# Forming the adaLN modulation's products on ScalarE and GpSimd instead of TensorE, in a two-layer RG-LRU and pooling trunk

## The chip, the cores and the metric

The kernel runs on one core of one Trainium2 chip. The core has TensorE (PE in the profile; its weight loads are listed apart as PEld), VectorE (DVE), ScalarE (ACT), GpSimd (POOL) and SyncE (SP), which issues nearly all DMAs here. The metric is the device time of one execution in microseconds (us); a time is a median over runs. The kernel before the change took 2298.68 us, median of 3 runs, from 2298.04 to 2298.79.

## The reference

The program is one pass of a small trunk over 640 tokens of width 1024: 512 latent tokens and 128 context tokens. There are two layers; each has a SwiGLU channel mixer, a token mixer (an RG-LRU with two scan directions in layer 0, a multi-window pool in layer 1), and another channel mixer. Each of these three sublayers is modulated by nine vectors per layer, which come from a conditioning vector:

```python
silu_ctx = jax.nn.silu(c_ctx)[None]
silu_lat = jax.nn.silu(c)
for l in range(DEPTH):
    mod_c = silu_ctx @ mod_w[l] + mod_b[l]     # [1, 1024] @ [1024, 9 * 1024]
    mod_s = silu_lat @ mod_w[l] + mod_b[l]
...
def _layer(x, mod, l, norm_g, ffn_w1, ffn_w3, ffn_w2, mixer):
    sh1, sc1, g1, sh2, sc2, g2, sh3, sc3, g3 = jnp.split(mod[:, None, :], N_MOD, axis=-1)
    h = _modulate(_rmsnorm(x, norm_g[l, 0]), sh1, sc1)
    x = x + 0.5 * g1 * _rmsnorm(_swiglu(h, ...), norm_g[l, 1])
    h = _modulate(_rmsnorm(x, norm_g[l, 2]), sh2, sc2)
    y, st = mixer(h)
    x = x + g2 * _rmsnorm(y, norm_g[l, 3])
    ...
```

Everything is float32. The change touches `silu_ctx @ mod_w[l]` and `silu_lat @ mod_w[l]`: two vectors (context and latent, called v = 0 and 1 in the kernel) against a matrix of 1024 x 9216 per layer.

## The kernel before, in words

The large products run as three float32r matmuls each (weights and activations are split exactly into a high and a low part: `wh`, `wl`; `gh`, `gl`; `hh`, `hl`). Weights come in pieces of 128 x 1024 through two buffers called `raw`; ScalarE makes `wh` (L137), VectorE makes `wl` (L138), and six pairs of them are kept ahead.

A channel mixer has 22 features of 128 rows. Per feature TensorE forms two products for token group A (256 tokens, `uvA`, two PSUM buffers) and two for group B (384 tokens, `uB` and `vB`, one PSUM buffer each), all at L326. ScalarE applies SiLU to u (L346), VectorE multiplies by v (L347), ScalarE and VectorE split the result into `gh` and `gl` (L153, L154). After every two features comes a block of 60 matmuls (`block_B`, L366) with the two features of the block before, whose sums go to `yacc` (L372 on ScalarE for the first block, L374 on VectorE after). The last four features are multiplied in `final`, tile by tile, with the norms behind them: `c_res` (a square with sum on ScalarE L280, an epsilon on VectorE L281, a power of -0.5 on GpSimd L283, two VectorE operations L291 and L292), the same statistic of x, a scaling on ScalarE (L298), and `c_h`, which transposes on TensorE (L431), modulates (L437, L439) and splits into `hh` and `hl` for the next sublayer. While the last tiles' norms finish, the next sublayer's first products of group A run.

The modulation of the first channel mixer is computed in `start`. The other 16 chunks of 1024 columns (shift, scale and gate, kinds 0, 1, 2, of the sublayers) come from a generator, `mod_gen`. It is stepped from the phases' code (`mod_step` once after each group of products, 9 steps at the start of a recurrent or channel mixer; `mod_until` before the chunk is needed). A chunk needs eight pieces of 128 x 1024, loaded into two buffers called `mw` on SP's queue; one step takes a piece and multiplies it with four matmuls of 128 x 32 weights and 256 columns, on four column groups of the array (L207). `csil` holds the two conditioning vectors' SiLU in columns 0 and 1 of 32. After eight steps the sums stand in PSUM (`m`, one buffer); a few small operations turn them into per-channel columns `ab` (kinds 0 and 1) or, by L249 and L252, into the broadcast gate `G` (kind 2), of which there is one buffer, so that a gate waits for the phase before to end.

Instructions stand on each engine's queue in an order that a scheduler sets when the program is built, each queue running in that order: an instruction that waits holds back all behind it on its engine. Work of the generator may stand on a queue well ahead of where the program text has it.

## Time and profile before

| | value |
|---|---|
| median of 3 runs | 2298.68 us |
| span of the profiled execution | 2297.5 us |
| PE busy, share of the span | 98% |
| PEld, DVE, ACT, POOL busy | 88%, 47%, 33%, 3% |
| granted TensorE clock, mean | 0.992 |
| DMA, mean of the span | 107 GB/s |

The profiled execution's own time is its span of 2297.5 us plus what lies around it, which the profile does not show; it is 1.2 us below the median of the runs. Busy times are unions of intervals, and matmuls overlap each other, so that a matmul's listed duration (0.28 us for 256 columns) is longer than its share of TensorE's time (one starts each 0.12 us). "Idle before" is what an engine waited for just ahead of an instruction, with the releaser behind the arrow. `x1024` for the modulation's matmuls at L207 counts two records per matmul: there are 512 of them, in 128 steps of four.

### The profile page before, as it was taken

The page shows a single profiled execution, that of the slowest core. Times are in us where ns is not written, and L with a number is a line of the kernel's source. Part 1 is how long each engine was busy: PE and PEld are TensorE (multiplying, and loading weights), DVE is VectorE, ACT ScalarE, POOL GpSimd, SP SyncE. Part 2 cuts the span into 40 slices and gives each one's busy share as a digit, 9 for nine tenths or more (in the row PEclk, how much of TensorE's full clock was granted, in tenths as well). Part 3 has the DMA queues.
Part 4 walks back from the last instruction along what each step waited for, and adds up shares of the span by engine and source line. Part 5 has one row for each costly group of instructions (what it writes and reads, how often), then busy time and mean ns, then how long its engine had stood idle before and what let it go on. Part 6 is the DMA issues. An engine that isn't in the chain of part 4 may idle for free.

```text
span 2297.5 us, 32647 instructions
## 1 busy us (share of the span) xinstructions
PE 2243.3 (98%) x14071; PEld 2024.6 (88%) x14071; DVE 1089.0 (47%) x1570; ACT 753.0 (33%) x1123; POOL 64.9 (3%) x107
## 2 busy tenths in 40 slices
PE   7999999998999999999999999999999899999998
PEld 5999889987888898989998898898897799999997
DVE  5333433346998643343344434334436743343444
ACT  5322112226976622112224421212125732222211
POOL 0000000000111000000000000000000100000000
PEclk9999999999999999999999999999999999999999
DMA  8333343324424344332221433433331322222221
GB/s 280 121 115 119 111 128 112 114 74 147 129 101 142 133 133 125 110 124 74 81 68 55 150 108 109 129 119 120 105 111 45 113 76 74 81 68 87 79 74 46
DMA packets 74288, 246.27 MB, mean 107 GB/s; under 512 B 7568, under 2 KB 15776, under 8 KB 74144
## 3 DMA queue, kind: packets, MB, share of 16 engines
q1 hardware_dynamic: 74112, 244.18, 33.6%
q8 instruction: 110, 1.80, 0.3%
q14 instruction: 34, 0.28, 0.0%
q0 software_dynamic: 32, 0.01, 0.0%
HBM read 238.91 MB, written 5.25 MB: 106 GB/s over the span
## 4 chain that ended last, share of the span: by engine, by line
PE 86%; DVE 6%; ACT 5%; DMA 2%; issue 1%; POOL 1%; SPq 0%; POOLq 0%; ACTq 0%; DVEq 0%
PE b L366 23%; PE uvA L326 22%; PE uB L326 17%; PE vB L326 16%; PE m L207 3%; ACT xp L280 2%; DVE yacc L291 1%; DVE x L292 1%; DVE yacc L374 1%; PE b L573 1%; POOL st L283 1%; DMA mw<-in_mod_w_dram 1%; ACT yacc L298 0%; PE b L746 0%; PE m L249 0%
## 5 line engine op out<-in xcount | busy, mean ns | idle before, releaser
L138 DVE TENSOR_TENSOR wl<-raw,wh 128x1024 fp32r<-128x1024 f32 x294 | 356.5, 1223 | 482.3 <-ACT wh L137 482.3
L137 ACT ACTIVATE wh<-raw 128x1024 fp32r<-128x1024 f32 x270 | 281.1, 1055 | 648.1 <-PE b L366 405.8
L326 PE MATMUL uvA<-hhA,wl 128*128 128x256 f32 x1536 | 440.2, 287 | 1.6 <-ACT xp L532 1.5
L326 PE MATMUL uvA<-hlA,wh 128*128 128x256 f32 x1536 | 435.8, 284 | 0.0
L326 PE MATMUL uvA<-hhA,wh 128*128 128x256 f32 x1536 | 435.3, 284 | 0.0
L366 PE MATMUL b<-wh,gl 128*128 128x512 f32 x960 | 376.6, 392 | 3.4 <-DVE gl L154 1.6
L366 PE MATMUL b<-wl,gh 128*128 128x512 f32 x960 | 375.0, 391 | 0.0
L366 PE MATMUL b<-wh,gh 128*128 128x512 f32 x960 | 374.3, 391 | 0.0
L374 DVE TENSOR_TENSOR yacc<-yacc,b 128x512 f32<-128x512 f32 x380 | 256.0, 686 | 169.7 <-PE b L366 169.6
L326 PEld LDWEIGHTS uvA<-hhA,wl 128*128 128x128 f32 x1536 | 294.3, 192 | 21.9 <-issue 15.4
L326 PEld LDWEIGHTS uvA<-hlA,wh 128*128 128x128 f32 x1536 | 294.8, 192 | 2.1 <-DVE hlB L154 0.4
L326 PEld LDWEIGHTS uvA<-hhA,wh 128*128 128x128 f32 x1536 | 294.7, 192 | 1.6 <-issue 1.6
L326 PE MATMUL uB<-hhB,wl 128*128 128x384 f32 x760 | 259.4, 341 | 0.9 <-ACT hhB L153 0.9
L326 PE MATMUL vB<-hhB,wl 128*128 128x384 f32 x760 | 254.8, 335 | 2.3 <-ACT gt L584 2.3
L326 PE MATMUL uB<-hlB,wh 128*128 128x384 f32 x760 | 254.9, 335 | 0.2
L326 PE MATMUL vB<-hhB,wh 128*128 128x384 f32 x760 | 255.0, 336 | 0.0
L326 PE MATMUL vB<-hlB,wh 128*128 128x384 f32 x760 | 254.9, 335 | 0.0
L326 PE MATMUL uB<-hhB,wh 128*128 128x384 f32 x760 | 254.6, 335 | 0.0
L366 PEld LDWEIGHTS b<-wh,gl 128*128 128x128 f32 x960 | 180.2, 188 | 48.0 <-issue 5.8
L366 PEld LDWEIGHTS b<-wh,gh 128*128 128x128 f32 x960 | 180.2, 188 | 37.6
L366 PEld LDWEIGHTS b<-wl,gh 128*128 128x128 f32 x960 | 180.3, 188 | 36.0
L347 DVE TENSOR_TENSOR r<-r,uvA 128x256 f32<-128x256 f32 x88 | 37.0, 421 | 266.6 <-ACT r L346 266.5
(207 smaller groups left out, 2389.5 us busy)
## 6 DMA issues: line engine op xcount, KB each, us to landing
raw<-in_w_dram SPq DMA_DIRECT2D x264, 512.0 KB, 3.5
mw<-in_mod_w_dram SPq DMA_DIRECT2D x132, 512.0 KB, 3.7
raw<-in_w_in_dram SPq DMA_DIRECT2D x16, 512.0 KB, 3.6
raw<-in_w_out_dram SPq DMA_DIRECT2D x8, 512.0 KB, 3.5
x_spill<-x SPq DMA_DIRECT2D x5, 512.0 KB, 2.6
x<-x_spill SPq DMA_DIRECT2D x5, 512.0 KB, 6.7
x<-in_x_s_dram SPq DMA_DIRECT2D x4, 512.0 KB, 6.3
wl<-in_mod_w_dram SPq DMA_DIRECT2D x4, 512.0 KB, 9.0
```

What stands on the lines that cost most here:

```text
L137: self.nc.scalar.activation(wh, raw, AF.Copy)
L138: self.nc.vector.tensor_sub(wl, raw, wh.bitcast(F32))
L207: nc.tensor.matmul(ps[32 * j:32 * j + 32, 0:256], self.csil[:, k, :], w[:, j * 256:(j + 1) * 256], start=(k == 0), stop=(k == KC - 1), til ...
L280: nc.scalar.activation(junk, src, AF.Square, scale=1.0 / 32.0, accum_out=ms)
L283: nc.gpsimd.tensor_tensor(rs, ms, self.mhalf, op=ALU.pow)
L291: nc.vector.scalar_tensor_tensor(y, y, rs, self.G[(l, s)][:, v], op0=ALU.mult, op1=ALU.mult)
L292: nc.vector.tensor_add(x, x, y)
L326: self.nc.tensor.matmul(out, a[:, sl], b[g][:, k], start=(n == 0), stop=(n == 3 * KC - 1))
L347: nc.vector.tensor_mul(su[:, cs], su[:, cs], v)
L366: nc.tensor.matmul(pb, a[:, ts_], b[:, ns], start=(c == 0), stop=(c == 3 * len(fl) - 1))
L374: nc.vector.tensor_add(y, y, pb)
L573: nc.tensor.matmul(pb, u[:, ws], v[:, a:b], start=(n == 0), stop=(n == 2))
```

## The change

The sum over a chunk's 1024 rows is split in two. The products of each weight element with the two conditioning numbers of its row, and their sum over the eight pieces, are formed elementwise in two accumulators of 128 x 1024 per chunk (`macc`, one per conditioning vector); TensorE then only sums the accumulators over their 128 partitions, with a matrix `onesel` that has one column of ones.

Per chunk a step still takes one piece, now loaded as two halves of 128 x 512. For each half ScalarE forms two products (an ACTIVATE Copy with a scale per partition). In the first step these go straight into the accumulators. In the other seven the product for v = 0 goes into a tile `mt` (one buffer), the product for v = 1 is written over the loaded half itself, and GpSimd adds both to the accumulators. The two `mw` buffers are now 128 x 512. Then one step issues eight matmuls (L222 of the changed kernel). A chunk has two more steps than before, one of them empty, and the 9 steps at the start of a mixer are now 2. The split gate rows share the tile `mt`. Over the whole program 512 matmuls in 128 steps go, and 128 matmuls in 16 steps, 512 ACTIVATEs and 448 GpSimd adds, each of 128 x 512, come; the 128 modulation loads of 512 KB become 256 loads of 256 KB.

```diff
-            "st": 12, "uvA": 2, "uB": 1, "vB": 1, "b": 3, "m": 1}
+            "st": 12, "macc": 2, "uvA": 2, "uB": 1, "vB": 1, "b": 3, "m": 1}
...
-            for k in range(KC):
+            for k in range(2 * KC):
                 items.append((l, part, k))
...
-            tl = self.t("mw", [P, D])
+            tl = self.t("mw", [P, 512])
             if k >= 0:
-                self.nc.sync.dma_start(tl, self.io["mod_w"][l, k * P:(k + 1) * P, part * D:(part + 1) * D])
+                c0 = part * D + (k % 2) * 512
+                self.nc.sync.dma_start(tl, self.io["mod_w"][l, (k // 2) * P:(k // 2 + 1) * P, c0:c0 + 512])
             else:
-                self.nc.sync.dma_start(tl[:, 0:512], self.io["grow"][3 * l + part // 3])
+                self.nc.sync.dma_start(tl, self.io["grow"][3 * l + part // 3])
...
         for (l, s, kind) in self.mod_order:
+            acc = [self.t("macc", [P, D]) for _ in range(2)]
+            for k in range(KC):
+                for h in range(2):
+                    w = self.mod_take()
+                    for v in range(2):
+                        o, sc = acc[v][:, h * 512:(h + 1) * 512], self.csil[:, k, v:v + 1]
+                        if k == 0:
+                            nc.scalar.activation(o, w, AF.Copy, scale=sc)
+                        else:
+                            pr = self.t("mt", [P, 512]) if v == 0 else w
+                            nc.scalar.activation(pr, w, AF.Copy, scale=sc)
+                            nc.gpsimd.tensor_add(o, o, pr)
+                    self.mod_dma()
+                yield
+            yield
             ps = self.p("m")
-            for k in range(KC):
-                w = self.mod_take()
+            for v in range(2):
                 for j in range(4):
-                    nc.tensor.matmul(ps[32 * j:32 * j + 32, 0:256], self.csil[:, k, :], w[:, j * 256:(j + 1) * 256],
-                                     start=(k == 0), stop=(k == KC - 1), tile_position=(0, 32 * j))
-                self.mod_dma()
-                yield
+                    nc.tensor.matmul(ps[32 * j:32 * j + 32, 0:256], self.onesel[:, v], acc[v][:, j * 256:(j + 1) * 256],
+                                     start=(v == 0), stop=(v == 1), tile_position=(0, 32 * j))
+            yield
...
-                mhl = self.t("mhl", [P, 2, 256], F32R)
+                mhl = self.t("mt", [P, 2, 256], F32R)
...
@@ ffn_start
-        self.mod_step(9)
+        self.mod_step(2)
@@ rg_start
-        self.mod_step(9)
+        self.mod_step(2)
...
-                    m = self.t("mw", [P, D]) if n < 2 else big[:, n - 2]
+                    m = self.t("macc", [P, D]) if n < 2 else big[:, n - 2]
...
+        self.onesel = self.t("onesel", [P, 2, 32])
+        nc.gpsimd.memset(self.onesel, 0.0)
+        for v in range(2):
+            nc.gpsimd.memset(self.onesel[:, v, v:v + 1], 1.0)
```

The rest of the diff takes comments out. Lines from `mod_gen` on stand 14 lines further down in the changed kernel, in `ffn_rest`, the norms and the phases alike (L326 is L340, L153 and above are unmoved).

The scheduler places the new work as follows. First TensorE, between two features of the first channel mixer. Before, one step of a chunk (`m`, from a piece in `mw`) stands between a block (`b`, L366) and the next feature's group A (`uvA`, L326):

```order
L366 MATMUL b_1101<-wh_695,gh_661 128x512
L207 MATMUL m_807<-mw_948,csil_68 32x256 x4
L326 MATMUL uvA_1115<-hhA_146,wl_933 128x256
L326 MATMUL uvA_1115<-hlA_148,wh_932 128x256
L326 MATMUL uvA_1115<-hhA_146,wh_932 128x256
```

With the change, the sum over partitions of a whole chunk (`macc`, two accumulators) stands between two features, and no other modulation product does:

```order
L340 MATMUL vB_3528<-hlB_153,wh_3267 128x384
L340 MATMUL vB_3528<-hhB_151,wh_3267 128x384
L222 MATMUL m_3583<-macc_2875,onesel_71 32x256 x4
L222 MATMUL m_3583<-macc_2876,onesel_71 32x256 x4
L340 MATMUL uvA_3592<-hhA_150,wl_3390 128x256
```

Per chunk, eight places of four matmuls became one of eight.

Second ScalarE, at the end of the first channel mixer of layer 1 (the last feature's SiLU, L346, the last weights `wh`, the last split `gh`, and the first square of the norms, L280). Before:

```order
L346 ACTIVATE r_14682<-uvA_14633 128x256
L346 ACTIVATE r_14682<-uB_14697 128x384
L137 ACTIVATE wh_15078<-raw_14689 128x1024
L137 ACTIVATE wh_15086<-raw_14695 128x1024
L153 ACTIVATE gh_14749<-r_14682 128x640
L280 ACTIVATE xp_14785,st_14786<-yacc_11526 128x1024
L280 ACTIVATE xp_14793,st_14794<-x_6586 128x1024
```

With the change (L360 is the SiLU, L294 the square; L214 are the products of a chunk, into `mt` and over the half in `mw`):

```order
L214 ACTIVATE mt_16181<-mw_16175,csil_68 128x512
L214 ACTIVATE mw_16175<-mw_16175,csil_68 128x512
L360 ACTIVATE r_15564<-uB_15588 128x384
L137 ACTIVATE wh_15977<-raw_15571 128x1024
L214 ACTIVATE mt_16188<-mw_16179,csil_68 128x512
L214 ACTIVATE mw_16179<-mw_16179,csil_68 128x512
L214 ACTIVATE mt_16195<-mw_16186,csil_68 128x512
L137 ACTIVATE wh_15985<-raw_15577 128x1024
L153 ACTIVATE gh_15640<-r_15564 128x640
L214 ACTIVATE mw_16186<-mw_16186,csil_68 128x512
L214 ACTIVATE mt_16202<-mw_16193,csil_68 128x512
L214 ACTIVATE mw_16193<-mw_16193,csil_68 128x512
```

Three products now stand between the last SiLU and the split `gh`, two ahead of that SiLU, and three behind `gh`, ahead of the first square, which is the next row.

Third GpSimd, in the norms right behind. Before, the powers of the norms (L283) follow each other:

```order
L283 TENSOR_TENSOR st_14789<-st_14786,mhalf_66 128x1
L283 TENSOR_TENSOR st_14797<-st_14794,mhalf_66 128x1
L283 TENSOR_TENSOR st_14832<-st_14829,mhalf_66 128x1
L283 TENSOR_TENSOR st_14840<-st_14837,mhalf_66 128x1
L283 TENSOR_TENSOR st_14915<-st_14912,mhalf_66 128x1
```

With the change (L297 is the power, L215 the adds):

```order
L297 TENSOR_TENSOR st_15688<-st_15685,mhalf_66 128x1
L215 TENSOR_TENSOR macc_16171<-macc_16171,mt_16209 128x512
L215 TENSOR_TENSOR macc_16172<-macc_16172,mw_16200 128x512
L215 TENSOR_TENSOR macc_16171<-macc_16171,mt_16216 128x512
L215 TENSOR_TENSOR macc_16172<-macc_16172,mw_16207 128x512
L297 TENSOR_TENSOR st_15696<-st_15693,mhalf_66 128x1
L215 TENSOR_TENSOR macc_16171<-macc_16171,mt_16223 128x512
L297 TENSOR_TENSOR st_15731<-st_15728,mhalf_66 128x1
L215 TENSOR_TENSOR macc_16172<-macc_16172,mw_16214 128x512
```

Adds now stand between the powers of one tile's two statistics and between tiles.

On ScalarE's queue the 512 products (L211 in a chunk's first step, L214 in the others) fall as follows: 131 in the first channel mixer of layer 0, 106 in its second, 136 in the first of layer 1 and 7 in its second; 60 among the recurrent mixer's own operations; 20 between the recurrent mixer and the next channel mixer's first products; 45 between the first channel mixer of layer 1 and the second, around the pool; and 7 where the first channel mixer ends. GpSimd's queue has 56 of the 448 adds among the recurrent mixer's operations, and 13 of the 16 sums over partitions stand in the channel mixers on TensorE's.

## Prediction

> **What bounds the kernel now.** I read the shares first, then the stages, then the chain that ended last.
>
> ```profile
> span 2297.5 us, 32647 instructions
> PE 2243.3 (98%) x14071; PEld 2024.6 (88%) x14071; DVE 1089.0 (47%) x1570; ACT 753.0 (33%) x1123; POOL 64.9 (3%) x107
> PE 86%; DVE 6%; ACT 5%; DMA 2%; issue 1%; POOL 1%; SPq 0%; POOLq 0%; ACTq 0%; DVEq 0%
> ```
>
> TensorE bounds it: 98% busy and 86% of the chain. ScalarE and GpSimd have room on average, so what counts is where that room lies. The next rows are busy time by stage (columns PE, PEld, DVE, ACT, POOL, then clock and DMA): first channel mixer, recurrent mixer, the norms behind it, second channel mixer, and two pieces around the pool.
>
> ```profile
> 62.00:485.00 423.00, 423.00 (x2692) 381.76 (x2692) 159.68 (x210) 95.78 (x132) 0.00 (x0) 1.00 0.37 114
> 545.00:740.00 195.00, 189.39 (x1250) 168.72 (x1251) 164.06 (x230) 148.77 (x224) 26.92 (x37) 0.98 0.42 133
> 740.00:800.00 60.00, 55.17 (x347) 46.88 (x345) 44.47 (x71) 39.15 (x64) 8.77 (x13) 1.00 0.37 125
> 800.00:1232.00 432.00, 432.00 (x2686) 396.95 (x2686) 171.14 (x224) 93.99 (x126) 0.00 (x0) 1.00 0.33 102
> 1735.00:1800.00 65.00, 60.38 (x370) 53.07 (x369) 44.30 (x72) 43.66 (x78) 6.03 (x11) 0.95 0.11 35
> 1800.00:1870.00 70.00, 64.03 (x439) 55.58 (x438) 42.32 (x68) 43.87 (x72) 5.81 (x9) 0.93 0.38 124
> ```
>
> In a channel mixer ScalarE is 22% busy and VectorE 38 to 40%: only TensorE limits. In the recurrent mixer VectorE is 84% and ScalarE 76% busy, and in the norms both stand near two thirds, in serial chains.
>
> **What leaves TensorE.** Two blocks of equal work, one with five modulation steps (40 records of L207, eight to a step) and one with none, then the steps by stage:
>
> ```profile
> 278.20:323.80 45.60, 3.19 (x40) 0.79 (x40) 1.00 0.42 127
> 1147.66:1189.48 41.82, 0.00 (x0) 0.00 (x0) 1.00 0.24 77
> 62.00:485.00 423.00, 20.45 (x256) 5.03 (x256) 1.00 0.37 114
> 545.00:740.00 195.00, 14.90 (x192) 4.83 (x192) 0.98 0.42 133
> 830.00:1232.00 402.00, 10.86 (x136) 2.67 (x136) 1.00 0.31 96
> 1310.00:1735.00 425.00, 21.73 (x272) 5.35 (x272) 1.00 0.38 114
> 26.05 1.30 PE L842 MATMUL m<-mw,csil 128*32 128x256 f32 x16 [2.64 <-issue]
> ```
>
> A step costs (45.60 - 41.82) / 5 = 0.756 us of the path, more than its 0.64 us busy. The three channel-mixer stages hold (256 + 136 + 272) / 8 = 83 steps, 62.7 us. The recurrent mixer holds 24 (18 us), and the transitions the other 21 (16 us). The new sum of eight matmuls has 16 records, as in the last row: 1.3 us, with its entry about 1.4. Thirteen of the 16 stand in channel mixers, 18 us. So TensorE's own gain there is 62.7 - 18 = **45 us**. Elsewhere I credit none: the recurrent mixer's other engines will set its pace (below), and in the transitions the steps filled time in which norms were finished.
>
> **What comes onto ScalarE, GpSimd and the load queue.** The prices nearest to the new operations:
>
> ```profile
> L153 ACT ACTIVATE hhB<-i 128x512 fp32r<-128x512 f32 x30 | 18.0, 630 | 1.7 <-DVE i L437 1.5
> L298 ACT ACTIVATE yacc<-x,st 128x1024 f32<-128x1024 f32 x30 | 34.2, 1143 | 5.6 <-POOL st L283 5.6
> L137 ACT ACTIVATE wh<-raw 128x1024 fp32r<-128x1024 f32 x270 | 281.1, 1055 | 648.1 <-PE b L366 405.8
> L283 POOL TENSOR_TENSOR st<-st,mhalf 128x1 f32<-128x1 f32 x60 | 34.9, 583 | 2050.3 <-DVE st L281 2043.0 <-DVE k_w L500 6.1 <-DVE k_w L510 1.3
> L154 DVE TENSOR_TENSOR hlB<-i,hhB 128x512 fp32r<-128x512 f32 x30 | 19.8, 688 | 5.6 <-ACT hhB L153 5.5
> mw<-in_grow_dram SPq DMA_DIRECT2D x6, 256.0 KB, 3.4
> ```
>
> A product is a 128x512 copy (0.63) plus what a scale per partition adds (1.143 - 1.055 = 0.09): 0.72 us, 512 of them 369 us. An add of 128x512 on GpSimd stands in no row. From below it is bounded by VectorE's own two-operand operation of that shape, 0.69; from above I take 2.6, that value with the waits shown below. I choose 1.2: the one-element power's 0.58 as fixed cost and 0.6 for 512 elements at VectorE's rate; it is nearest to the power, which is the only two-operand row on that engine. The Trainium skill, "GPSIMD Engine Reference", section "3.1 Elementwise — side-by-side cycle accounting", gives 4497 ns for an add of 2048 elements, a quarter of which is 1.12 as an estimate; by it the sum below would be some 5 us lower.
>
> The pace of a chunk follows from its two `mw` buffers. A buffer comes free only when GpSimd has added the product that lies in it. So per step: load 3.4, first product 0.72, two adds 2.4, hand-offs 0.3 (my allowance): **6.8 us** (5.8 at the low add price). Products stand in ScalarE's fixed order; while one waits for its load or for `mt`, the SiLU, `wh` and `gh` behind it wait too.
>
> In the channel mixers there is cover:
>
> ```profile
> 1119.51 5.75 PE uvA L326 x48
> 1125.26 4.17 PE uB L326 x24
> 1133.59 5.75 PE uvA L326 x48
> 1147.66 13.67 PE b L366 x60
> ```
>
> A feature takes 14.1 us. The u of group B is whole at 1129.4 and its bank is wanted again at 1139.3, so its SiLU may be 9.4 us late (9.9 less 0.5). The changed queue puts up to four steps in a feature, 27 us of pace against 14.1; but the lag builds over two features, and the second is followed by the block's 13.7 us, in which ScalarE has little else. Stepped through with 6.8, the SiLUs come 5 to 8 us late, just inside. The first block's evictions on ScalarE, and chunks that start in the second feature, can exceed it. I take 1 us per chunk, **+12 us** (0 to 35).
>
> On SP's queue the smaller loads number 128 more, and each now waits for an add; the weight loads (`raw`) stand in order behind them, and behind those the `wh` and `wl` of later features. I cost this at nothing: of the 648 us that ScalarE was idle before `wh` (L137 above), 406 ended when a block freed a pair, so weights are split as soon as there is room, six pairs (one block, 42 us) ahead of their use; less the 14 us that a feature holds its own pair, 28 us are left. With that cover gone, each weight load behind a held one would cost TensorE the step's pace, 6.8 us.
>
> **The recurrent mixer.** GpSimd's one-element copies there show who waits for whom. The rows are a short and a long copy (GpSimd), and what VectorE ran meanwhile:
>
> ```profile
> 640.89 0.70 POOL L616 COPY nst<-i 128x1 f32<-128x1 f32 x1 [0.47 <-DVE i L614]
> 641.46 1.29 DVE L370 COPY yacc<-b 128x512 f32<-128x512 f32 x2
> 723.83 6.52 POOL L616 COPY nst<-x 128x1 f32<-128x1 f32 x1 [0.47 <-DVE x L614]
> 728.74 1.56 DVE L589 TENSOR_TENSOR i<-i,xc 128x642 f32<-128x642 f32 x2
> 730.22 0.42 DVE L235 TENSOR_TENSOR mrow<-m,mw 128x256 f32<-128x256 f32 x1
> L138 DVE TENSOR_TENSOR wl<-raw,wh 128x1024 fp32r<-128x1024 f32 x23 | 28.0, 1218 | 0.0
> L626 DVE TENSOR_TENSOR i<-i,gt 128x128 f32<-128x128 f32 x3 | 0.9, 287 | 0.0
> ```
>
> Each copy ends just after VectorE starts an operation that reads PSUM; during a run on SBUF operands one element took 6.52 us. The Trainium skill, "SBUF — State Buffer", section "Who interferes with whom", says that a VectorE instruction with two SBUF inputs and a GpSimd instruction that reads SBUF exclude each other, and who starts first keeps the pair; these rows agree. VectorE's two-SBUF-operand groups in this stage, 24 of them with the last two rows first and last, sum to 140 us. With 56 adds at 1.2 that is 140 + 67 = 207 against a stage of 195; ScalarE gets 149 + 60 x 0.72 = 192. Waits in both directions come on top: I take **+20 us** (-3 if the adds cost 0.69 and slip in, +60 if each takes 2.6).
>
> **The transitions.** At the end of layer 1's first channel mixer:
>
> ```profile
> 1729.90 0.49 ACT L346 ACTIVATE r<-uB 128x384 f32<-128x384 f32 x1 [3.72 <-PE uB L326]
> 1735.03 0.72 ACT L153 ACTIVATE gh<-r 128x640 fp32r<-128x640 f32 x1
> 1740.49 1.06 ACT L280 ACTIVATE xp<-yacc 128x1024 bf16<-128x1024 f32 x1 [4.75 <-DVE yacc L374]
> 1759.03 1.06 ACT L280 ACTIVATE xp<-x 128x1024 bf16<-128x1024 f32 x1 [0.50 <-DVE x L292]
> ```
>
> Now five products that need new loads stand ahead of that `gh`: counted forward from the SiLU of group A, loads at 1731.2, 1732.6 and 1738.0 put it at 1739.8, 5 us late, and TensorE's last products wait for it. Between the two squares quoted, 18.5 us apart, twelve products now stand; six halves at 3.4 are 20 us, partly under other waits: +8. The pool's gate is summed last: adds 2.4, sum 1.4, small operations and four broadcasts about 6, of which I count +6. Some 24 products in the pool's norms and 20 behind the recurrent mixer cost +8 each in the same way, with powers queued behind adds on GpSimd. Together **+35 us** (10 to 60).
>
> **Sum.** -45 + 12 + 20 + 35 = +22 on the profiled 2297.5, which is 1.2 below the median: **2321 us**, slower by 1%.
>
> **Rivals.** (1) The adds run near 0.69 and rarely wait. Pace 5.8, recurrent mixer at 140 + 39 = 179 under its 195, channel-mixer lag +3, transitions +15: -45 + 3 + 0 + 15 = -27, **2272**. For it: GpSimd is 3% busy, VectorE 38% in channel mixers. Against: the 6.52 us copy. It decides if an add with its waits stays under about 0.9. (2) Adds starve behind VectorE's runs, 2.6 each in recurrent mixer and transitions: +60 and +55 instead of 20 and 35, so -45 + 12 + 60 + 55 = +82, **2380**. For it: that copy; against: VectorE idles more once ScalarE is late, which lets adds in. (3) Costs come to half of mine and return just the gain: **2298**.
>
> **How the numbers follow.** Forecast 0.50 (own range 2304 to 2350), rival 1 0.23, rival 2 0.16, rival 3 0.11. A change under 0.2% cannot be told from none. Faster is rival 1, 0.23; same is rival 3, 0.11; slower the rest, 0.66. The range leaves out the outer parts of rivals 1 and 2: 2268 to 2375.
>
> **What would show it.** Channel-mixer blocks near 42 us with small waits of TensorE on ScalarE's SiLU confirm the gain and the cover; blocks near 50 refute the cover. Mean of L215: 1.2 confirms, 0.7 or 2.6 speak for rivals 1 and 2. VectorE's two-operand groups should grow in the recurrent mixer, its stage should pass 205 us, and the last split and the squares around the pool should start late by the numbers above. If that stage and the transitions keep their lengths, the forecast is wrong and the kernel faster.

## The result, and the profile after

The changed kernel takes 2408.33 us, median of 3 runs (2407.84 to 2410.0), against 2298.68: a ratio of 1.0476, 95% interval 1.0457 to 1.0495. It is slower by 110 us. I had forecast 2321, slower by 22, with a range to 2375: the sign was right, the size was a fifth.

The head of the changed kernel's page (span, shares of the engines, the chain that ended last):

```profile
span 2406.6 us, 32594 instructions
PE 2217.3 (92%) x13303; PEld 2043.9 (85%) x13303; DVE 1194.0 (50%) x1570; ACT 1082.1 (45%) x1626; POOL 686.3 (29%) x558
PE 61%; DVE 10%; ACT 9%; POOL 7%; DMA 7%; issue 6%; SPq 0%; POOLq 0%; ACTq 0%; DVEq 0%
```

TensorE does less, yet it is idle for 189 us of the span (54 before), and its share of the chain fell from 86% to 61%. VectorE, to which the change gave nothing, is busy 105 us longer. The groups that were new or that grew (busy us, mean ns, idle before), and, last, `wl` in the kernel before:

```profile
L215 POOL TENSOR_TENSOR macc<-macc,mt 128x512 f32<-128x512 f32 x224 | 320.6, 1431 | 900.8 <-ACT mt L214 897.6 <-PE vB L445 2.4
L215 POOL TENSOR_TENSOR macc<-macc,mw 128x512 f32<-128x512 f32 x224 | 320.0, 1429 | 48.6 <-ACT mw L214 48.5
L138 DVE TENSOR_TENSOR wl<-raw,wh 128x1024 fp32r<-128x1024 f32 x294 | 409.3, 1403 | 551.2 <-ACT wh L137 543.8 <-PE b L380 7.2
L214 ACT ACTIVATE mt<-mw,csil 128x512 f32<-128x512 f32 x224 | 161.7, 722 | 243.2 <-DMA mw<-in_mod_w_dram 203.2 <-POOL macc L215 39.9
```

```profile
L138 DVE TENSOR_TENSOR wl<-raw,wh 128x1024 fp32r<-128x1024 f32 x294 | 356.5, 1223 | 482.3 <-ACT wh L137 482.3
```

An add costs 1.43 us with its waits, a product 0.72. The costliest waits of TensorE (us in total, times, longest). The first row (49.5 of its 52.4 us) and the last lie in the blocks of the three channel mixers that hold modulation steps; there the profile of the kernel before shows no wait of TensorE for an eviction. The second row lies in the norms, the third in the recurrent mixer. The two rows behind are the whole of the first and the second kind in the kernel before:

```profile
PE b L380 <- DVE yacc L388: 52.4, 10, 10.4
PE uB L445 <- ACT yacc L312: 38.1, 17, 11.0
PE b L587 <- ACT r L588: 11.7, 3, 4.6
PE b L380 <- ACT yacc L386: 9.2, 1, 9.2
```

```profile
PE b L366 <- DVE yacc L374: 0.8, 1, 0.8
PE uB L431 <- ACT yacc L298: 7.5, 12, 2.0
```

By stages, before and then after. A stage ends where the next one's first square of `yacc` or first SiLU of group B starts; the rows are the recurrent mixer and the pool with its norms, then the first channel mixer, for each kernel (columns as in the prediction's windows):

```profile
505.71:750.86 245.15, 231.06 (x1472) 202.62 (x1471) 202.32 (x288) 178.90 (x273) 35.26 (x51) 0.99 0.40 130
1740.49:1848.20 107.71, 97.12 (x654) 82.60 (x653) 73.53 (x123) 77.52 (x134) 11.84 (x20) 0.92 0.22 71
62.00:505.71 443.71, 443.71 (x2817) 401.04 (x2817) 167.73 (x220) 100.98 (x139) 0.00 (x0) 1.00 0.37 113
```

```profile
521.77:804.41 282.64, 236.18 (x1306) 210.75 (x1305) 237.56 (x285) 209.76 (x330) 122.81 (x109) 0.91 0.31 99
1818.30:1954.96 136.66, 98.31 (x598) 86.75 (x597) 91.13 (x123) 103.45 (x178) 77.21 (x61) 0.85 0.25 74
62.00:521.77 459.77, 430.42 (x2617) 401.24 (x2617) 177.15 (x219) 186.46 (x265) 145.27 (x112) 0.97 0.35 109
```

Over the whole program the three channel mixers that hold steps lost 33 us (16 + 11 + 6), where I had forecast a gain of 33; the recurrent mixer lost 37 (forecast 20); the norms and the pool between mixers lost 37 (forecast 35); the rest 2.

**One block, row by row.** VectorE, GpSimd, ScalarE and TensorE of the changed kernel around 240 us, each in its own order:

```profile
240.43 1.93 DVE L138 TENSOR_TENSOR wl<-raw,wh 128x1024 fp32r<-128x1024 f32 x1 [7.37 <-ACT wh L137]
246.53 1.92 DVE L138 TENSOR_TENSOR wl<-raw,wh 128x1024 fp32r<-128x1024 f32 x1 [3.71 <-ACT wh L137]
248.36 0.81 DVE L154 TENSOR_TENSOR gl<-r,gh 128x640 fp32r<-128x640 f32 x1
249.10 1.27 DVE L388 TENSOR_TENSOR yacc<-yacc,b 128x512 f32<-128x512 f32 x2
240.00 1.27 POOL L215 TENSOR_TENSOR macc<-macc,mw 128x512 f32<-128x512 f32 x1
246.09 1.26 POOL L215 TENSOR_TENSOR macc<-macc,mw 128x512 f32<-128x512 f32 x1
235.46 0.72 ACT L214 ACTIVATE mt<-mw,csil 128x512 f32<-128x512 f32 x1 [2.86 <-DMA mw<-in_mod_w_dram]
239.35 1.04 ACT L137 ACTIVATE wh<-raw 128x1024 fp32r<-128x1024 f32 x1
244.07 0.72 ACT L214 ACTIVATE mt<-mw,csil 128x512 f32<-128x512 f32 x1 [0.99 <-DMA mw<-in_mod_w_dram]
245.45 1.04 ACT L137 ACTIVATE wh<-raw 128x1024 fp32r<-128x1024 f32 x1
235.13 0.39 PE L380 MATMUL b<-wh,gl 128*128 128x512 f32 x1
239.02 0.39 PE L380 MATMUL b<-wh,gh 128*128 128x512 f32 x1
249.83 0.79 PE L380 MATMUL b<-wh,gl 128*128 128x512 f32 x1 [10.42 <-DVE yacc L388]
250.42 0.63 PE L380 MATMUL b<-wl,gh 128*128 128x512 f32 x1
253.94 0.39 PE L380 MATMUL b<-wl,gh 128*128 128x512 f32 x1
```

Two things are to be seen. First the **order**: TensorE fills its three `b` banks from 235.13 to 239.4 us and then waits 10.42 us for an eviction. VectorE was idle for about half of that time; but the evictions stand on its queue behind the `wl` and `gl` of the second feature, and these waited for `wh`, which stood on ScalarE's queue behind products that waited for loads and adds. Second the **exclusion**: `wl` takes 1.22 us alone, here 1.93 and 1.92. The adds that started at 240.00 and 246.09 ended at 241.27 and 247.35, and each `wl` ended 1.09 and 1.10 us after that: it got going about when the add was done.

### The profile page after: what moved, and what is told of

It reads as the page before. It is cut to its first block, busy times and chain, and to the rows that moved or that the text cites. A ratio compares the mean times of both kernels' runs of the same rounds, so it can differ in the third digit from the quotient of the medians.

```text
span 2406.6 us, 32594 instructions
## 1 busy us (share of the span) xinstructions
PE 2217.3 (92%) x13303; PEld 2043.9 (85%) x13303; DVE 1194.0 (50%) x1570; ACT 1082.1 (45%) x1626; POOL 686.3 (29%) x558
## 4 chain that ended last, share of the span: by engine, by line
PE 61%; DVE 10%; ACT 9%; POOL 7%; DMA 7%; issue 6%; SPq 0%; POOLq 0%; ACTq 0%; DVEq 0%
PE b L380 20%; PE uvA L340 15%; PE uB L340 12%; PE vB L340 11%; POOL macc L215 6%; DMA mw<-in_mod_w_dram 6%; DVE wl L138 2%; ACT mt L214 2%; ACT xp L294 2%; DVE yacc L305 1%; DVE x L306 1%; POOL st L297 1%; ACT wh L137 1%; ACT yacc L312 1%; DVE yacc L388 1%
## 5 line engine op out<-in xcount | busy, mean ns | idle before, releaser
L138 DVE TENSOR_TENSOR wl<-raw,wh 128x1024 fp32r<-128x1024 f32 x294 | 409.3, 1403 | 551.2 <-ACT wh L137 543.8
L215 POOL TENSOR_TENSOR macc<-macc,mt 128x512 f32<-128x512 f32 x224 | 320.6, 1431 | 900.8 <-ACT mt L214 897.6
L380 PE MATMUL b<-wh,gl 128*128 128x512 f32 x960 | 387.0, 403 | 71.0 <-DVE yacc L388 52.4
L340 PE MATMUL uvA<-hhA,wl 128*128 128x256 f32 x1536 | 440.0, 287 | 9.0 <-ACT gt L597 2.9
L340 PE MATMUL uvA<-hlA,wh 128*128 128x256 f32 x1536 | 439.7, 286 | 0.5 <-DVE hlA L154 0.4
L340 PE MATMUL uvA<-hhA,wh 128*128 128x256 f32 x1536 | 438.5, 286 | 0.0
L380 PE MATMUL b<-wl,gh 128*128 128x512 f32 x960 | 384.2, 400 | 0.0
L380 PE MATMUL b<-wh,gh 128*128 128x512 f32 x960 | 382.4, 399 | 0.0
L215 POOL TENSOR_TENSOR macc<-macc,mw 128x512 f32<-128x512 f32 x224 | 320.0, 1429 | 48.6 <-ACT mw L214 48.5
L340 PEld LDWEIGHTS uvA<-hhA,wl 128*128 128x128 f32 x1536 | 297.8, 194 | 16.7 <-issue 5.8
L340 PEld LDWEIGHTS uvA<-hlA,wh 128*128 128x128 f32 x1536 | 298.4, 194 | 3.1 <-DVE hlA L154 1.4
L340 PEld LDWEIGHTS uvA<-hhA,wh 128*128 128x128 f32 x1536 | 298.2, 194 | 0.8 <-issue 0.8
L380 PEld LDWEIGHTS b<-wh,gl 128*128 128x128 f32 x960 | 186.1, 194 | 117.4 <-DVE yacc L388 56.5
L214 ACT ACTIVATE mt<-mw,csil 128x512 f32<-128x512 f32 x224 | 161.7, 722 | 243.2 <-DMA mw<-in_mod_w_dram 203.2
L340 PE MATMUL uB<-hhB,wl 128*128 128x384 f32 x760 | 258.2, 340 | 5.9 <-ACT hhB L153 5.9
L340 PE MATMUL uB<-hlB,wh 128*128 128x384 f32 x760 | 256.7, 338 | 2.1 <-DVE hlB L154 2.1
L340 PE MATMUL uB<-hhB,wh 128*128 128x384 f32 x760 | 256.4, 337 | 0.0
L340 PE MATMUL vB<-hhB,wl 128*128 128x384 f32 x760 | 254.3, 335 | 0.0
L340 PE MATMUL vB<-hlB,wh 128*128 128x384 f32 x760 | 254.1, 334 | 0.0
L340 PE MATMUL vB<-hhB,wh 128*128 128x384 f32 x760 | 254.1, 334 | 0.0
```

The costliest lines, as they stand in the source:

```text
L138: self.nc.vector.tensor_sub(wl, raw, wh.bitcast(F32))
L214: nc.scalar.activation(pr, w, AF.Copy, scale=sc)
L215: nc.gpsimd.tensor_add(o, o, pr)
L340: self.nc.tensor.matmul(out, a[:, sl], b[g][:, k], start=(n == 0), stop=(n == 3 * KC - 1))
L380: nc.tensor.matmul(pb, a[:, ts_], b[:, ns], start=(c == 0), stop=(c == 3 * len(fl) - 1))
```

## The experiments

The theories at the start: A, the fixed orders with the pace of a step through load, product and add; B, the exclusion of VectorE and GpSimd; C, ScalarE's mere work. "Moved" below is how many of ScalarE's 1533 ACTIVATEs must at least be put elsewhere to turn the changed kernel's order into that of the run, read from the two traces by operation, tiles and shape.

**First set.** No adds:

```diff
-                            nc.gpsimd.tensor_add(o, o, pr)
```

> The changed kernel without GpSimd's adds: the products on ScalarE, their loads and TensorE's last sums stay; left out is the sum over the chunks after the first. Three theories. A, order: `wh` and `gh` stand behind products that wait for loads and adds (6.6 us a step), VectorE's `wl`/`gl` wait for them, and the block's evictions of `yacc` wait behind those. Without adds a half buffer is free again after load 2.7 + two products 1.4 + hand-offs 0.3, so a step costs about 4.5 us instead of 6.6: TensorE's waits for `yacc` in the channel mixers fall from 62 us to under 20, these mixers go from +35 to about -15 against before, the recurrent mixer from +37 to +10 and the transitions from +37 to +20: 2315 us (2295 to 2335). B, shared SBUF access: VectorE is slowed by the adds; without them its `wl` is back at 1.22 us and the whole gain appears, 2255 to 2270. C, capacity: the 369 us of products on ScalarE are what costs; 2390 to 2408.

No products after the first step:

```diff
-                            pr = self.t("mt", [P, 512]) if v == 0 else w
-                            nc.scalar.activation(pr, w, AF.Copy, scale=sc)
-                            nc.gpsimd.tensor_add(o, o, pr)
+                            nc.gpsimd.tensor_add(o, o, w)
```

> The changed kernel without ScalarE's products after the first chunk of eight: GpSimd adds the loaded weights themselves, so 448 of the 512 products and the scaling by the conditioning vector are left out; loads, adds and TensorE's sums stay. A (order): nothing stands ahead of `wh` and `gh`, so TensorE's waits for `yacc` in the channel mixers go, and these come out at about -40 against before; recurrent mixer +20 and transitions +15 stay through the adds: 2290 us (2275 to 2305). B (VectorE slowed by the adds): as the changed kernel, 2380 to 2410, `wl` still at 1.40 us. C (ScalarE's capacity): 2255 to 2270.

Two memsets in place of an add, then three:

```diff
-                            nc.gpsimd.tensor_add(o, o, pr)
+                            nc.gpsimd.memset(pr, 0.0)
+                            nc.gpsimd.memset(pr, 0.0)
```

> The changed kernel with each add replaced by two memsets of the product's 128x512 tile on GpSimd, about as long together (the 128x256 memset took 0.311 us in before's trace, so 1.1 to 1.3 us for two of 128x512): the hand-offs ScalarE to GpSimd to load stay, but GpSimd reads no SBUF operand; left out is the sum over chunks. A (order): the pace stays 6 to 6.6 us a step and the time stays within 2385 to 2412, though `wl` falls from 1.40 to about 1.22 us. B (VectorE slowed by adds that read SBUF): 2255 to 2300. C (capacity): 2390 to 2408, as A.

> The changed kernel with each add replaced by three memsets of 128x512 (0.53 us each in the run with two, so 1.6 us against the add's 1.43 with its waits): the hand-offs are at least as slow as with adds, about 7.0 us a step where the adds gave 6.4, but nothing on GpSimd reads SBUF; left out is the sum over chunks. If the step's pace through the fixed orders of ScalarE and of the load queue is what costs (pace), the time is that of the changed kernel or worse, 2395 to 2450 us, and TensorE's waits for `yacc` come back to 50 us. If it is that adds and VectorE's operations exclude each other (exclusion), `wl` stays at 1.22 us and the time at 2270 to 2310.

Measured: no adds 2254.2 us (ratio 0.9802, 0.9786 to 0.9818); no products 2432.6 (1.0577, 1.0561 to 1.0593); two memsets 2275.8 (0.9890, 0.9876 to 0.9905); three memsets 2282.9 (0.9925, 0.9909 to 0.9942). C fell: the kernel without adds keeps all of ScalarE's products and is faster than the kernel before, and without products it was no faster. Without products the three mixers did go from +33 to -9 us, the way A has it, but the recurrent mixer with the norms behind it went from +47 to +86. Read alone, the memsets seemed to settle it for B, since three of them took longer than an add. That reading was premature: in these four kernels the scheduler had moved 87 (no adds) to 246 (three memsets) of ScalarE's ACTIVATEs, and without adds the last sum of a chunk no longer waited for GpSimd.

**Edits of single links.** The splits on VectorE in the bodies of the channel mixers, and the modulation's loads on GpSimd's queue:

```diff
-            if self.dve_lo <= i < self.dve_hi:
+            if self.on_dve or self.dve_lo <= i < self.dve_hi:
...
-        self.split(gh, gl, src)
+        if self.on_dve:
+            self.nc.vector.tensor_copy(gh, src)
+            self.nc.vector.tensor_sub(gl, src, gh.bitcast(F32))
+        else:
+            self.split(gh, gl, src)
```

> The changed kernel complete, with the copies `wh` and `gh` in the four channel mixers' bodies made by VectorE in place of ScalarE, so that nothing on VectorE ahead of the block's evictions waits for ScalarE but the SiLU's product. A (order): TensorE's waits for `yacc` (52 us with L388's 20 + 14 + 15 and more) fall under 10 us, the channel mixers go from +35 against before to between -25 and 0, the rest stays: 2355 us (2340 to 2380). B (VectorE slowed by adds): VectorE gets some 200 us more work on SBUF operands and the waits grow: 2408 to 2440. C (ScalarE's capacity): relieved of about 210 us of copies, gains the like of A; told apart by the waits of SiLU on ScalarE, which C lets fall too and A does not.

```diff
-                self.nc.sync.dma_start(tl, self.io["mod_w"][l, (k // 2) * P:(k // 2 + 1) * P, c0:c0 + 512])
+                self.nc.gpsimd.dma_start(tl, self.io["mod_w"][l, (k // 2) * P:(k // 2 + 1) * P, c0:c0 + 512])
```

> The changed kernel complete, with the modulation's loads issued from GpSimd's queue instead of SyncE's, so that a weight load (`raw`) never stands behind a load that waits for an add. If the order of the load queue, which my prediction cost at nothing, is part of the loss: 30 us or more less than the changed kernel, 2340 to 2380. If only ScalarE's order and the exclusion count: 2400 to 2420, as the changed kernel.

Splits on VectorE: 2394.7 us (1.0409, 1.0393 to 1.0424), outside every range that I had written. The scheduler's order changed with it. The mixers went from +33 to +17 and not to the forecast gain. TensorE's waits for `yacc` only fell to 35 us. SiLU still stands behind the products, and VectorE's next operation waits for it up to 11.9 us (first row, us, times, longest; at most 4.5 us in the changed kernel); that this is what kept the waits up was not shown. Loads on GpSimd's queue: 2498.9 us (1.0862, 1.0845 to 1.0878), worse by 90 and also outside both ranges; each issue now takes 0.56 us of GpSimd (second row), and 197 of ScalarE's ACTIVATEs moved.

```profile
DVE r L362 <- ACT r L361: 272.4, 83, 11.9
```

```profile
L189 POOL DMA_DIRECT2D mw<-in_mod_w_dram x256 | 142.3, 556 | 797.6 <-ACT macc L211 708.5 <-POOL macc L215 62.9 <-ACT r L360 9.1
```

So neither edit alone took the loss away, and since both changed the order too, neither says what its link is worth. What the load queue cost is read from the waits, under "Why the prediction was right or wrong".

**Shorter adds, and half of them.**

```diff
-                            nc.gpsimd.tensor_add(o, o, pr)
+                            for q in range(2):
+                                cs = slice(q * 256, (q + 1) * 256)
+                                nc.gpsimd.tensor_add(o[:, cs], o[:, cs], pr[:, cs])
```

> The changed kernel complete, with each add of 128x512 on GpSimd made as two of 128x256. If VectorE's operations wait for the add that is under way (exclusion), the longest such wait falls from 1.26 to about 0.65 us, the mean of `wl` from 1.40 to about 1.31 us, and about half of the 125 us that separate adds from memsets come back: 2345 us (2325 to 2375). If what costs is the total time that GpSimd holds SBUF, not the length of one add: 2395 to 2425.

```diff
-                            nc.gpsimd.tensor_add(o, o, pr)
+                            if v == 0:
+                                nc.gpsimd.tensor_add(o, o, pr)
+                            else:
+                                for _ in range(3):
+                                    nc.gpsimd.memset(pr, 0.0)
```

> The changed kernel with one of each two adds (that of the context's vector, v = 1) replaced by three memsets of 1.6 us in all; left out is that half of the sum. Hand-offs and pace stay at least as slow, the number of operations on GpSimd that read SBUF is halved. Exclusion: about half way between 2283 (three memsets) and 2408 (adds): 2345 us (2325 to 2370). A threshold in the pace: at one of the two ends.

Adds in halves: 2459.9 us (1.0698, 1.0682 to 1.0714). Here the order is nearly the changed kernel's (5 moved). B's forecast of `wl` held, at 1.32 us, and its forecast of the time failed: the kernel became 52 us slower, more than the other branch allowed too.

```profile
L217 POOL TENSOR_TENSOR macc<-macc,mw 128x256 f32<-128x256 f32 x448 | 408.8, 933 | 42.4 <-ACT mw L214 42.2
L138 DVE TENSOR_TENSOR wl<-raw,wh 128x1024 fp32r<-128x1024 f32 x294 | 385.3, 1321 | 591.4 <-ACT wh L137 584.5 <-DMA mw<-in_mod_w_dram 6.7
```

Two halves take 1.78 us against 1.43, and a step in a dense chunk 7.0 to 7.5 us against 6.3 to 7.0 (twice the mean time from one product in `mt` to the next). So pace counts in this order. Half the adds: 2375.3 us (1.0323, 1.0307 to 1.0338), between the ends but not half way, with 121 moved; I draw nothing more from it.

**Order and operation apart.** Four more kernels hold the order fixed. A table with each engine's order of another kernel is laid over the program as edges that order instructions and wait for nothing (shown here without the reading of the table):

```diff
+        info = mybir.DependencyInfo(mybir.DependencyClass.NoSync, mybir.DependencyReason.DATA)
...
+                if prev is not None:
+                    self.tc.add_manual_dep(mine[at], prev.name, info, reason="order")
+                prev = mine[at]
```

The memsets now also touch the accumulator, so that the last sum waits for GpSimd as it does with adds:

```diff
-                            nc.gpsimd.tensor_add(o, o, pr)
+                            nc.gpsimd.memset(pr, 0.0)
+                            nc.gpsimd.memset(pr, 0.0)
+                            nc.gpsimd.memset(o, 0.0)
```

> Each add replaced by two memsets of the product's tile and one of the accumulator's half (0.53 us each, so the last sum still waits for GpSimd); left out is the sum over chunks. By edges that order instructions without waiting, ScalarE, VectorE, SyncE and TensorE run in exactly the order of the changed kernel. Exclusion (VectorE and the adds hold each other off): no SBUF operand is read on GpSimd, so 2270 to 2310 us, `wl` 1.22. Order and pace (a step of about 7.2 us against 6.6, in the changed kernel's order): 2400 to 2460 us with waits of TensorE for `yacc` of 50 us or more, though `wl` is 1.22.

> The changed kernel complete, adds as they are, with ScalarE's and SyncE's instructions in exactly the order that the scheduler gave the kernel of the run with memsets on tile and accumulator (335 of ScalarE's rows moved against the changed kernel). Exclusion: 2390 to 2420 us, as the changed kernel, `wl` 1.40. Order: the order itself was the loss, 2285 to 2330 us.

> As the run with memsets on tile and accumulator, but in the order that the scheduler gives it; left out is the sum over chunks. It shows what the sum's lost dependency was worth in the run with three memsets (2283 us): if nothing, 2280 to 2290; if the transitions had gained by it (the last sum before the pool waits for GpSimd again), 2295 to 2320.

> The changed kernel without adds, in exactly the changed kernel's order on ScalarE, VectorE, SyncE and TensorE; left out is the sum over chunks. A step's pace falls to about 5 us and nothing on GpSimd reads SBUF. Exclusion: 2250 to 2265 us, as without adds in the other order. Order alone: 2380 to 2410 us. Order with pace: between, about 2300.

A fifth holds the product's tile for an add's length, in the changed kernel's order:

```diff
-                            nc.gpsimd.tensor_add(o, o, pr)
+                            nc.gpsimd.memset(pr, 0.0)
+                            nc.gpsimd.memset(pr, 0.0)
+                            nc.gpsimd.memset(pr[:, 0:256], 0.0)
+                            nc.gpsimd.memset(o[:, 0:8], 0.0)
```

> As the run with memsets in the changed kernel's order, but the product's tile is held as long as an add held it: two memsets of 128x512 (0.53 us each), one of 128x256 (0.31) and one of 8 columns of the accumulator, 1.4 us together against the add's mean of 1.43; left out is the sum over chunks. A step should take 6.5 to 7.0 us against the changed kernel's 6.3 to 6.7. What is still missing to 2408 us is then the exclusion. If it was worth the whole 52 us: 2350 to 2360. If half of these were pace: 2375 to 2385. If all: 2400 to 2415.

Measured, in us (ratios to the kernel before, with intervals, in the order of the rows, left to right: 1.0476; 1.0415, 1.0399 to 1.0430; 1.0236, 1.0218 to 1.0255; 1.0007, 0.9993 to 1.0021; 1.0265, 1.0246 to 1.0284; 0.9820, 0.9805 to 0.9834; 0.9802):

| on GpSimd | the changed kernel's order | an order the scheduler gave without adds |
|---|---|---|
| adds | 2408.3 | 2395.8 (ScalarE and SyncE alone in that order) |
| memsets, 1.6 us a product, tile free after 1.06 | 2355.7 | 2300.6 |
| memsets, 1.4 us a product, tile held as long | 2361.0 | not run |
| nothing | 2258.9 | 2254.2 (its own order) |

The first memsets in the changed kernel's order fell between the two ranges that I had written for them; those of equal length came out 1 us above the range in which all that is missing to the adds is exclusion. The run without adds fell into the range for exclusion; alone it doesn't tell, because without adds the hand-off is gone too. The memsets in their own order take 18 us more than the three memsets of the first set, which left the last sum free; the order differs as well, so what that wait is worth by itself stays open.

The left column separates the causes, since ScalarE, VectorE, SyncE and TensorE stand in one order there (GpSimd's was not laid down). Pages and groups of the last two kernels of that column, first the memsets of equal length, then no adds:

```profile
PE 2208.3 (93%) x13303; PEld 2036.8 (86%) x13303; DVE 1091.0 (46%) x1570; ACT 1080.8 (46%) x1626; POOL 684.9 (29%) x1902
L146 DVE TENSOR_TENSOR wl<-raw,wh 128x1024 fp32r<-128x1024 f32 x294 | 356.1, 1222 | 577.6 <-ACT wh L145 577.4
PE b L391 <- DVE yacc L399: 45.1, 12, 9.1
522.88:789.00 266.12, 229.77 (x1308) 205.49 (x1307) 204.36 (x285) 209.53 (x331) 121.21 (x295) 0.94 0.32 103
```

```profile
PE 2174.7 (96%) x13303; PEld 2012.9 (89%) x13303; DVE 1090.2 (48%) x1570; ACT 1077.8 (48%) x1626; POOL 67.8 (3%) x110
486.73:728.16 241.43, 221.89 (x1308) 198.75 (x1307) 201.62 (x285) 208.96 (x331) 36.95 (x51) 0.98 0.35 114
```

GpSimd is busy 684.9 us with the memsets and 686.3 with the adds, and a dense step takes 6.3 to 7.0 us in both. VectorE is back at 1091 us and `wl` at 1.222, so memsets, which read nothing, do not hold `wl` off. Yet TensorE still waits 45 us for `yacc`. From this:

- TensorE's steps gone, products and loads added: 2258.9 - 2298.7 = **-40 us**.
- The hand-off through GpSimd, at the adds' length and in the fixed order, with the last sum's wait for GpSimd: 2361.0 - 2258.9 = **+102 us**.
- Adds that read SBUF in place of memsets, the exclusion: 2408.3 - 2361.0 = **+47 us**.

The four runs with memsets of equal length lie between 2356.8 and 2366.5, so that the last two figures hold to about 5 us.

By stages, from the profiled spans, against before (the spans give 110 and 42 us in place of 102 and 47, since the profiled run with memsets of equal length took 5.5 us more than its median, and that without adds 2.2 less; a row can miss its sum by 1 through rounding):

| stage | no adds | hand-off adds | exclusion adds | changed kernel |
|---|---|---|---|---|
| three channel mixers | -51 | +79 | +4 | +33 |
| recurrent mixer | -4 | +25 | +17 | +37 |
| norms and pool | +10 | +6 | +21 | +37 |
| last mixer, end | +2 | 0 | 0 | +2 |

A and B are both right, each in its own place. An add takes 1.33 us in the mean of the first channel mixer and 1.70 in the recurrent mixer: there the two engines hold each other off more. The order is worth 55 us where memsets hand off, 13 with adds and 5 with nothing. In the three mixers alone it is worth more: with adds they lose 9 us in the other order in place of 33, and with memsets they gain 29 in place of losing 18; with adds the other stages give 12 of that back. So the order decides how much of the pace reaches TensorE there. It can't be said what the exclusion would cost in the other order with equal lengths, since that pair was not run.

**The change in the bodies alone, and another engine for it.** Outside the bodies TensorE's steps are left as before; inside, the accumulators are formed by the change's method, or by VectorE in one operation per vector:

```diff
+                if self.in_body:
...
+                        if init:
+                            nc.vector.tensor_scalar(o, w, sc, None, op0=ALU.mult)
+                        else:
+                            nc.vector.scalar_tensor_tensor(o, w, sc, o, op0=ALU.mult, op1=ALU.add)
```

> The kernel before, complete, with the steps that fall in the four channel mixers' bodies formed by VectorE alone as two multiply-adds of 128x1024 (about 1.29 us each by VectorE's rate on SBUF operands), summed over partitions by TensorE as in the change; all other steps stay on TensorE. No ScalarE product, no GpSimd add. Exclusion and pace both: no GpSimd work and no hand-off between engines, so TensorE's gain of 83 x 0.756 = 63 us less 14 sums of 1.4 appears: 2260 us (2248 to 2280). If VectorE's multiply-adds of 2.6 us a step delay the evictions (three banks cover 4.1 us): 2280 to 2310.

> The kernel before, complete, with the change's own method (products on ScalarE, adds on GpSimd, last sum on TensorE) only for the steps that fall in the channel mixers' bodies, and TensorE's steps elsewhere; loads are whole 128x1024 pieces as before. If the stages' costs are each their own: bodies +35 as in the changed kernel, recurrent mixer and transitions at 0: 2334 us (2310 to 2345). If the bodies lose through what the other stages leave late: under 2299.

2308.0 us (1.0033, 1.0020 to 1.0046) and 2432.3 (1.0576, 1.0560 to 1.0591): both missed the forecast, and both at one place. (2308 lies in the range that I had written for delayed evictions, but TensorE's waits for these were 17 us, less than those below.) I had given the accumulators the buffers named `a`, which the pool's scale vectors hold from the third mixer's start to the pool. The steps of that mixer could not run and piled up ahead of the pool; in the kernel with VectorE TensorE waited for them there:

```profile
PE m L291 <- DVE a L218: 37.0, 3, 18.5
```

With the scale vectors elsewhere:

```diff
-            sc = self.t("a", [P, 512])
+            sc = self.t(("gt", "xc")[h], [P, 512])
```

> As the kernel with VectorE's multiply-adds in the channel mixers' bodies, complete, with the pool's two scale vectors moved from the buffers named `a` to those named `gt` and `xc`: there they no longer hold the accumulators' buffers from the third channel mixer's start to the pool, which had pushed 50 of that mixer's multiply-adds into the pool's stage. The first two channel mixers keep their -17 and -11, the third comes to about -18, the pool's stage from +56 back to 0: 2255 us (2245 to 2265). If VectorE's multiply-adds and not the buffers delayed the pool's stage: 2290 to 2310.

> As the kernel with the change's method in the channel mixers' bodies alone, complete, with the pool's scale vectors moved as in the run beside it. The first two mixers keep +25 and +10, the third comes to between +5 and +10, recurrent mixer and transitions stay within 3 of before: 2343 us (2330 to 2355). If the loss in the pool's stage (+119) came from the adds themselves: 2400 or more.

The change's method in the bodies: 2347.8 us (1.0207, 1.0190 to 1.0224). The three mixers lose 25 + 10 + 20 = 55 us, the other stages are within 2 of before (for the third mixer I had written 5 to 10). So the mixers lose by themselves, not through what other stages leave late. VectorE in the bodies: 2250.0 us, ratio **0.9789, 0.9775 to 0.9804**, faster than both kernels. Its page, its multiply-adds, and its wait of TensorE for evictions:

```profile
span 2246.9 us, 31864 instructions
PE 2193.9 (98%) x13583; PEld 2017.0 (90%) x13583; DVE 1272.3 (57%) x1740; ACT 753.9 (34%) x1123; POOL 65.5 (3%) x110
L218 DVE SCALAR_TENSOR_TENSOR a<-mw,csil,a 128x1024 f32<-128x1024 f32 x146 | 181.9, 1280 | 24.2 <-DMA mw<-in_mod_w_dram 23.8
PE b L403 <- DVE yacc L411: 2.8, 4, 1.3
```

VectorE's busy time grows by 183 us (1089.0 to 1272.3) for 85 steps, and it waits only 24 us for its loads; the mixers gain 20 + 11 + 21 = 51 us, and no other stage moves by more than 1. What ScalarE and GpSimd did with four products, four adds and a hand-off for each in a step is here two operations of one engine, whose loads come ahead of time.

## Why the prediction was right or wrong

- **TensorE's own gain, -45: right.** With the adds gone and the order unchanged the three mixers are 51 us shorter, 6 more than forecast.
- **The prices: nearly right.** Product 0.72, as predicted. An add with no VectorE operation in its way takes 1.26 to 1.30 us, 1.43 in the mean, where I took 1.2. A step of 6.8 us was forecast; dense chunks run at 6.3 to 7.0. That this fits is partly luck: a load lands after 2.7 us (3.4 forecast), and two adds take 2.9 (2.4 forecast).
- **The cover in the channel mixers, +12 (0 to 35): the step that failed.** At the pace I forecast, the hand-off cost 79 us there in place of 12: 67 of the 87 us by which the sum missed. The sentence that failed is that a feature's lag is covered since "the second is followed by the block's 13.7 us, in which ScalarE has little else". I looked only at ScalarE's SiLU and TensorE's `uB` bank; there the cover held, and in these three mixers TensorE waits for `uB` nowhere. The block needs VectorE for its evictions, and on VectorE's queue these stand behind `wl` and `gl`, which wait for ScalarE. The cover is three `b` banks: 18 matmuls that start 0.23 us apart, 4.1 us. The row with 10.42 us shows it. Each such wait costs again behind it (see the last section).
- **The load queue, at nothing: borne out for the weights.** The run that moved the loads says little, as it changed the order and loaded GpSimd as well. But in the changed kernel ScalarE waits no longer for weight loads than before (changed kernel first, then before); SyncE's queue order was not varied by itself.

```profile
ACT wh L137 <- DMA raw<-in_w_dram: 4.7, 5, 1.6
ACT wh L137 <- DMA raw<-in_w_dram: 5.2, 5, 2.5
```

- **The recurrent mixer, +20: too small at +37, and only partly for the reason given.** I summed VectorE's and GpSimd's times as if they excluded each other. That is 17 us by the runs; VectorE's busy time there grew from 202 to 238 us, and an add took 1.70 us there in place of 1.2. Another 25 us are hand-off, which I had left out of this stage.
- **The transitions, +35: right at +37 as a sum, by other terms.** I gave most of it to the pace of loads and products. Products and loads cost 10, the hand-off 6, the exclusion 21. That the sum agrees is luck.
- **The rivals.** The first fell, since adds run at 1.43 and its mixers' lag of 3 us was 79. The second came nearest (2380, 28 us short) for a wrong reason: adds take 1.70 us in the recurrent mixer and 1.59 in the pool's norms, not 2.6. It left out the mixers, as I did. The third fell: the costs were more than mine, not half.

## What to carry to other kernels

Before work is moved to engines with room, write down for the busiest engine's every releaser what stands ahead of it on its own in-order queue, and what that waits for; the cover is the shortest bank of buffers on the way, not the idle share. A chain of three engines and a load per item puts its pace into all of their queues; one fused operation on one engine with its input loaded ahead does not. And when an experiment swaps an operation in a kernel that a scheduler orders, compare the orders first: a cheap stand-in can win by the order that it was given.

## What the runs showed of the hardware

**Exclusion by the instruction.** A VectorE operation on two SBUF operands waits for a GpSimd add in progress to end (the two `wl` of 1.92 and 1.93 us), but not for memsets: `wl` is 1.222 us in the mean of a kernel with 1792 of them. The Trainium skill, "SBUF — State Buffer", section "Who interferes with whom", says that such an instruction contends with a GpSimd instruction that reads SBUF and not with one that only writes it; both runs agree. In the recurrent mixer it also reached operations such as these, changed kernel first, then the memsets of equal length:

```profile
L567 DVE SCALAR_TENSOR_TENSOR xc<-xp,cols,xc 128x642 f32<-128x642 f32 x12 | 13.4, 1119 | 0.3
L135 DVE CAST wh<-raw 128x1024 fp32r<-128x1024 f32 x24 | 21.4, 901 | 2.3 <-DMA raw<-in_w_out_dram 1.8 <-DMA raw<-in_w_in_dram 0.4
```

```profile
L578 DVE SCALAR_TENSOR_TENSOR xc<-xp,cols,xc 128x642 f32<-128x642 f32 x12 | 10.6, 884 | 0.3
L143 DVE CAST wh<-raw 128x1024 fp32r<-128x1024 f32 x24 | 17.4, 735 | 8.5 <-DMA raw<-in_w_out_dram 7.2 <-DMA raw<-in_w_in_dram 1.3
```

The cast has a single SBUF input and grew too, from 0.735 to 0.901 us; I had counted two-operand groups only. In the kernel before it takes 0.688 us, and 0.689 in the fixed order without adds, so that the memsets may have held it up a little as well, unlike `wl`.

**A wait of TensorE costs twice.** Behind the 10.42 us wait eight matmuls start 0.43 us apart before the usual 0.23 returns; the granted clock is 0.50 from 249.8 to 253.4 us and 0.99 right behind. The changed kernel's TensorE is busy 2217.3 us with the same 13303 records that take 2174.7 without adds in the same order; the mean granted clock is 0.963 against 0.989. The Trainium skill, "TensorE: Matmul & The Clock Gate", section "Part 1: The HAM clock gate (the "warmup" mystery)", states half rate after an idle window; the spacing and the clock here agree. So 43 us more of busy time stand beside the waits themselves.
